# Gathering the experts' tokens for several turns at once, in split products

## The chip, the cores and the metric

The kernel runs on one core of a Trainium2 chip. The metric is the device time of one execution in microseconds (us), and smaller is better. The engines of the core are named as the profile names them: PE (TensorE, its matrix products), PEld (its loads of the stationary operand), DVE (VectorE), ACT (ScalarE), POOL (GpSimd), SP (SyncE, which here only issues the transfers of the weights, in order, on one queue).

## The reference, cut to what matters

Two layers of a small transformer work on 256 tokens of width 1024. The second layer ends with a mixture of eight experts, of which each token uses two:

```python
def moe_swiglu(h, router_w, w1, w3, w2):
    t = h.reshape(B * L, D)                       # 256 x 1024
    logits = (t @ router_w).astype(jnp.float32)
    top_v, top_i = lax.top_k(logits, TOP_K)       # 2 of 8
    gates = jax.nn.softmax(top_v, axis=-1)
    combine = jnp.einsum('tk,tke->te', gates, jax.nn.one_hot(top_i, N_EXPERTS, dtype=jnp.float32))
    out = jnp.zeros_like(t)
    for e in range(N_EXPERTS):
        out = out + combine[:, e:e + 1] * swiglu(t, w1[e], w3[e], w2[e])
    return out.reshape(B, L, D)
...
        hx = modulate(rmsnorm(x, norm_ffn_w[l]), sh2x, sc2x)
        x = x + g2x * channel_mixer(hx, l, ...)
```

An expert's `w1` and `w3` are 1024 x 3584 and its `w2` is 3584 x 1024, all in float32: 42 MiB (44 MB) an expert, 352 MB for the eight. Everything that comes ahead of the experts (modulation, mixers, the dense layer) is left as it is.

## The kernel before

The last half of the execution is `expert_pass`: eight **turns**, one for each expert, in an order that the kernel works out itself (`plan`). A turn holds the tokens of one expert in 128 slots (turns 0, 2, 4 and 6, **long**) or in 64 (turns 1, 3, 5 and 7, **short**); `TURNS` and `short(e)` say which. The busiest experts get the long turns. In the text behind this, a turn is named by its number e.

The weights of a turn come in 42 **units** of 1 MiB (`load_unit`, line 128): four chunks of the hidden width, of each first the units of `w1` and `w3` (`up`), and then, one chunk later, those of `w2` (`down`). A unit lands in one of the 8 KiB-a-partition buffers of the list `places["raw"]`. They are taken in turn: two of `hbq`, the four `rr` of the ring, `raw6` to `raw{NRM - 1}` of the pool `wm`, and for a while the places of tiles that are not needed yet (`macc` three times, `hg1` once). With NRM = 12 that is twelve buffers in the steady state. SP issues the transfer of a unit as soon as its buffer is free, so the number of buffers is how far the transfers can run ahead of the products.

In a long turn the products are float32 by splitting: ACT writes the rounded high part `hi` of a unit (line 1691), DVE the rest `lo` = raw - hi (line 1702), and PE multiplies high by high, high by low and low by high with operands of the type float32r (lines 1599, 1600 and 1603; `mm3`, lines 156 to 158, for the downs). The buffer of the unit is free when `lo` is written. In a short turn PE takes the unit as it is, in float32 (lines 1591 and 1623), in pairs of half arrays, and the buffer is free when PE has done with it; ACT and DVE have little to do then.

`fill()` and the loop behind it set the order of the instructions. For each unit: its products; then the high part of a unit two ahead (AHI = 2) and the low part of the next one (ALO = 1); then one step (`pull(behind_work[0], 1)`) of the work that waits in the list `behind_work`, first in, first out; then a step of each chunk in work (`chunk`: silu times the other branch, and the transposes of the result for the downs). All operations of `dv` and `av` keep the order in which they are written (class `InOrder`), so DVE and ACT run in the order of the program; almost all their rows in the expert part have line 177.

Ahead of its products a turn needs its tokens in its slots, transposed: `HG[e]`. `gather(e)` makes them. DVE writes a matrix `oh` (256 tokens by slots) that holds, at a token's slot, the reciprocal of its norm, and zero elsewhere; PE multiplies the residual `resid[2 + t]` by it in float32 (line 1392 for a short turn, 1405 for a long one, 16 products in each), and ACT applies scale and bias of the modulation from PSUM (and makes the high part, DVE the low one, for a long turn). `gather(e + 1)` is put into `behind_work` in the third chunk of turn e (line 1547), so the tokens of the short turns 1, 3, 5 and 7 are gathered in a long turn, and those of the long turns 2, 4 and 6 in a short one. The first turn's are gathered ahead of the pass. `finish(e, y)` brings the result back to the tokens: it transposes `oh` on PE (line 1436), takes where it is positive, and multiplies; it runs in the turn after e. In a short turn the 64 slots stand twice in `oh`, since the two halves of the result lie on partitions 0 to 63 and 64 to 127.

## Time and profile before

| what | value |
|---|---|
| median of 3 runs | 1666.03 us (1665.50 to 1667.06) |
| the profiled execution | 1667.27 us, span of its instructions 1665.5 us |
| busy share of the span: PE, DVE, ACT | 96 %, 63 %, 44 % |
| time of the chain that ended last: PE, DMA, DVE, ACT | 83 %, 6 %, 6 %, 3 % |
| moved by DMA | 479.06 MB, 288 GB/s over the span |
| DMA from about the 22nd of 40 slices on | tenths 9, 384 to 415 GB/s |

The page gives shares of the whole span, but the kernel has two parts: to about 786 us PE is busy and the DMA engines are half used (163 GB/s or so in many slices), and in the pass of the experts both are near their limits. So the stretches have to be read one by one. Times are counted from the start of the span. "Granted clock" is that of TensorE as a share of its full 2.4 GHz; 0.5 is 1.2 GHz. A busy PE is not a PE at its peak: the ends of matrix products are modelled and overlap, so the spacing of their starts is what counts.

### The profile page before, as it was taken

The numbers are of one execution on the slowest core, as the hardware profiler recorded it, in microseconds if no ns is written. First come the engines' busy times: TensorE is split into PE (matmuls) and PEld (weight loads), VectorE is DVE, ScalarE is ACT, GpSimd is POOL, SyncE is SP. The second block draws the span as 40 slices with busy tenths as digits, with TensorE's granted clock in tenths as the row PEclk, the third lists the DMA queues.
The fourth block names the chain that finished last, engine by engine and source line by source line (L and its number), as shares of the span: only waits on it lengthen the run. The fifth ranks groups of instructions, "written<-read, shape, count | busy, mean of one in ns | idle before, by whom it ended". The sixth has DMA issues, their size and how long they took to land.

```text
span 1665.5 us, 21562 instructions
## 1 busy us (share of the span) xinstructions
PE 1606.3 (96%) x8150; PEld 1159.5 (70%) x8150; DVE 1046.6 (63%) x1314; ACT 726.1 (44%) x892; POOL 27.5 (2%) x54
## 2 busy tenths in 40 slices
PE   7989999999999999999999999999999999999995
PEld 3868888788888888877786357874478844578532
DVE  3798897888567656866995127862178820588322
ACT  4733455322321347554775036741267611567201
POOL 1000000000000000000000000000000000000000
PEclk9999999999999999999999999999999999999997
DMA  9534385565666544546999999999999999999995
GB/s 372 160 102 136 96 267 163 163 189 171 189 190 201 156 128 140 174 154 240 332 357 318 415 406 413 407 406 407 409 412 409 410 390 408 410 414 406 384 405 201
DMA packets 186586, 479.06 MB, mean 288 GB/s; under 512 B 11585, under 2 KB 64961, under 8 KB 171873
## 3 DMA queue, kind: packets, MB, share of 16 engines
q1 hardware_dynamic: 185040, 473.80, 77.1%
q10 hardware_dynamic: 1074, 2.72, 0.5%
q8 instruction: 68, 1.11, 0.3%
q0 software_dynamic: 352, 1.00, 0.2%
q14 instruction: 52, 0.43, 0.1%
HBM read 476.43 MB, written 1.05 MB: 287 GB/s over the span
## 4 chain that ended last, share of the span: by engine, by line
PE 83%; DMA 6%; DVE 6%; ACT 3%; issue 1%; SPq 1%; DVEq 0%; ACTq 0%
PE h L1591 11%; PE mm L156 8%; PE mm L157 8%; PE mm L158 8%; PE h L1600 6%; PE h L1603 6%; PE h L1599 6%; PE y L156 5%; PE y L157 5%; PE y L158 5%; PE y L1623 4%; DMA rr<-moe_w 3%; PE sc L598 1%; PE sc L1570 1%; DVE lo L149 1%
## 5 line engine op out<-in xcount | busy, mean ns | idle before, releaser
L145 ACT ACTIVATE hi<-raw 128x1024 fp32r<-128x1024 f32 x127 | 134.6, 1059 | 303.2 <-PE mm L157 100.3
L177 DVE TENSOR_TENSOR rb<-raw,rb 128x2048 fp32r<-128x2048 f32 x73 | 167.1, 2290 | 80.2 <-ACT rb L177 60.5
L149 DVE TENSOR_TENSOR lo<-raw,hi 128x1024 fp32r<-128x1024 f32 x127 | 155.2, 1223 | 80.3 <-ACT hi L145 78.9
L419 DVE SCALAR_TENSOR_TENSOR rr<-rr,cs,rr 128x512 f32<-128x512 f32 x256 | 181.9, 747 | 9.6 <-DMA rr<-b_mod 4.6
L1600 PE MATMUL h<-rb,hg 128*128 128x512 f32 x448 | 177.2, 396 | 4.5 <-DVE rb L177 4.4
L156 PE MATMUL mm<-hbk,hi 128*128 128x512 f32 (+1 forms) x456 | 166.5, 366 | 1.1 <-DVE tm L837 1.0
L157 PE MATMUL mm<-hbk,hi 128*128 128x512 f32 (+1 forms) x456 | 163.6, 359 | 0.5 <-DVE hbk L310 0.5
L158 PE MATMUL mm<-hbk,lo 128*128 128x512 f32 (+1 forms) x456 | 163.8, 359 | 0.0
L177 ACT ACTIVATE rb<-raw 128x2048 fp32r<-128x2048 f32 x73 | 139.9, 1917 | 51.0 <-PE h L1603 31.8
L1591 PE MATMUL h<-raw,hgs 128*64 128x512 f32 (+1 forms) x720 | 143.4, 528 | 0.0
L177 DVE TENSOR_TENSOR sil<-sil,h 128x512 f32<-128x512 f32 (+1 forms) x44 | 29.1, 662 | 165.7 <-PE h L1591 148.5
L1599 PE MATMUL h<-rb,hg 128*128 128x512 f32 x288 | 109.1, 399 | 1.4 <-ACT rb L177 1.4
L1591 PEld LDWEIGHTS h<-raw,hgs 128*64 128x64 f32 x720 | 51.6, 137 | 77.5 <-issue 69.3
L1600 PEld LDWEIGHTS h<-rb,hg 128*128 128x128 f32 x448 | 85.1, 190 | 26.7 <-DVE rb L177 6.9
L177 DVE TENSOR_TENSOR rb<-raw,part 128x2048 fp32r<-128x2048 f32 x42 | 96.1, 2288 | 10.1 <-PE h L1600 4.6
L156 PEld LDWEIGHTS mm<-hbk,hi 128*128 128x128 f32 x456 | 85.9, 189 | 16.6 <-issue 2.7
L177 DVE TENSOR_TENSOR rb<-rr,rb 128x2048 fp32r<-128x2048 f32 x35 | 80.0, 2288 | 27.7 <-ACT rb L177 24.1
L177 ACT ACTIVATE part<-raw 128x2048 fp32r<-128x2048 f32 x42 | 80.4, 1914 | 36.2 <-DMA raw<-moe_w 16.8
L157 PEld LDWEIGHTS mm<-hbk,hi 128*128 128x128 f32 x456 | 86.0, 189 | 14.1 <-issue 1.0
L158 PEld LDWEIGHTS mm<-hbk,lo 128*128 128x128 f32 x456 | 86.0, 189 | 13.0
L1603 PE MATMUL h<-rb,hg 128*128 128x512 f32 x288 | 88.6, 393 | 2.5 <-DVE hg L177 2.5
L157 PE MATMUL y<-rb,ht 128*128 128x512 f32 x224 | 87.6, 391 | 0.0
(381 smaller groups left out, 2967.9 us busy)
## 6 DMA issues: line engine op xcount, KB each, us to landing
raw<-moe_w SPq DMA_DIRECT2D x212, 1024.0 KB
rr<-moe_w SPq DMA_DIRECT2D x110, 1024.0 KB
rr<-w_mod SPq DMA_DIRECT2D x80, 512.0 KB
raw<-ffn_w SPq DMA_DIRECT2D x72, 512.0 KB
raw<-w_in SPq DMA_DIRECT2D x32, 512.0 KB
raw<-w_out SPq DMA_DIRECT2D x23, 512.0 KB
raw<-moe_w SPq DMA_DIRECT2D x12, 512.0 KB
rb<-w_mod SPq DMA_DIRECT2D x5, 1024.0 KB
```

Source lines behind the costliest of these rows:

```text
L145: ins = nc.scalar.activation(hi, raw, AF.Copy).ins
L149: nc.vector.tensor_tensor(lo, raw, hi.bitcast(F32), op=OP.subtract)
L156: nc.tensor.matmul(ps, lh, rh, start=start, stop=False)
L157: nc.tensor.matmul(ps, lh, rl, start=False, stop=False)
L158: nc.tensor.matmul(ps, ll, rh, start=False, stop=stop)
L177: r = getattr(self.engine, name)(*args, **kw)
L419: nc.vector.scalar_tensor_tensor(accs[x], rv[:, k, :], cs[:, x * 8 + kb:x * 8 + kb + 1], accs[x], op0=OP.mult, op1=OP.add)
L1591: nc.tensor.matmul(H[i][0][x * 64:x * 64 + 64, :n], HG[e][:, k0 + j, :], hi[:, j, x * n:(x + 1) * n], start=(k0 + j == 0), stop=(k0 + j == 7))
L1599: nc.tensor.matmul(H[i][b], hgh[:, kb, :], hi[:, j, bc], start=(kb == 0), stop=False)
L1600: nc.tensor.matmul(H[i][b], hgh[:, kb, :], lo[:, j, bc], start=False, stop=False)
L1603: nc.tensor.matmul(H[i][b], hgl[:, kb, :], hi[:, j, bc], start=False, stop=(kb == 7))
L1623: nc.tensor.matmul(Y[e][0][hh * 64:hh * 64 + 64], ht[:, j0 + j, half], hi[:, j, xc], start=on, stop=off)
```

## The change

`gather` stays for the passes that run only if an expert has more tokens than slots (they are not run on these inputs), and without its branch for short turns. In the main pass `gather_group(es)` takes its place, twice: for the turns 1 to 3, put into `behind_work` in the second chunk of turn 0, and for the turns 4 to 7, in the second chunk of turn 3. It writes one matrix of zeros and ones for all their slots (64 + 64 + 128 = 256 columns, and 64 + 64 + 128 + 128 = 384), and multiplies the residual by the reciprocal norm first, split in a high part `xh` (ACT) and a low part `xl` (DVE), 256 of its columns at a time; each of the 8 blocks of 128 features then needs four products in float32r, high and low for two halves of the tokens (line 1440 of the changed kernel). ACT writes the short turns' tokens of a block in one instruction, and the high part of each long turn's; DVE writes each long turn's float32 value and its low part. The tokens of all turns of a group stay until they are used, so there are new tiles `hgs0`, `hgs1` (4 KiB a partition each) and wider `ohg0`, `ohg1`; NRM falls from 12 to 11. In `finish` the matrix of a short turn has its 64 columns once, and two products with the unit matrix for each half of the tokens (four in all) take the place of two transposes. A short turn's chunk waits one unit longer before its transposes (`yield`).

```diff
-NRM, NHM, NLM, AHI, ALO = 12, 3, 2, 2, 1
+NRM, NHM, NLM, AHI, ALO = 11, 3, 2, 2, 1
...
-            if short(e):
-                HG[e] = hg = mb.tile([128, KB, 64], F32, name="hgs", tag=f"hg{e % 2}")
-                ps = scps()
-                for k4 in range(2):
-                    for kb in range(4 * k4, 4 * k4 + 4):
-                        for t in range(2):
-                            nc.tensor.matmul(ps[:, kb * 64:(kb + 1) * 64], resid[2 + t][:, kb * 128:(kb + 1) * 128],
-                                             oh[:, t, 0:64], start=(t == 0), stop=(t == 1))
-                    yield
-                for kb in range(KB):
-                    av.activation(hg[:, kb, :], ps[:, kb * 64:(kb + 1) * 64], AF.Identity,
-                                  scale=AXM[0][:, kb:kb + 1], bias=AXM[1][:, kb:kb + 1])
-                return
...
+        def gather_group(es):
+            es = sorted(es, key=lambda e: rooms_of[e])
...
+            i = es[0] // 4
+            oh = (rxp, mo)[i].tile([128, 2, n], F32R, name="ohg", tag=f"ohg{i}")
+            for e in es:
+                cols_ = slice(starts[e], starts[e] + rooms_of[e])
+                OH[e] = oh[:, :, cols_].bitcast(F32)
+                for t in range(2):
+                    dv.tensor_scalar(oh[:, t, cols_], iota[:, 0:rooms_of[e]], PM(t, e), None, op0=OP.is_equal)
+            yield
+            ns = sum(short(e) for e in es)
+            hs = mb.tile([128, KB, ns, 64], F32, name="hgs", tag=f"hgs{i}")
...
+                hg = mb.tile([128, 2, KB, 128], F32R, name="hg", tag=f"hg{e // 2 % 2}")
+                HG[e] = hg[:, 0], hg[:, 1]
+            for k2 in range(4):
+                fc = slice(k2 * 256, (k2 + 1) * 256)
+                xh, xl = (mb.tile([128, 2, 256], F32R, name=x, tag="ys", bufs=2) for x in ("xh", "xl"))
+                for t in range(2):
+                    av.activation(xh[:, t], resid[2 + t][:, fc], AF.Copy, scale=nM.ys[2 + t])
+                    dv.scalar_tensor_tensor(xl[:, t], resid[2 + t][:, fc], nM.ys[2 + t], xh[:, t].bitcast(F32),
+                                            op0=OP.mult, op1=OP.subtract)
+                yield
+                for j in range(2):
...
+                    for x in (xh, xl):
+                        for t in range(2):
+                            nc.tensor.matmul(ps[:, :n], x[:, t, jc], oh[:, t, :], start=(x is xh and t == 0),
+                                             stop=(x is xl and t == 1))
+                    yield
+                    ak, bk = AXM[0][:, kb:kb + 1], AXM[1][:, kb:kb + 1]
+                    av.activation(hs[:, kb].rearrange("p a b -> p (a b)"), ps[:, :ns * 64], AF.Identity, scale=ak, bias=bk)
+                    h32 = mo.tile([128, 2, 128], F32, name="h32", tag="oht")
+                    for k, e in enumerate(longs):
+                        pe_ = ps[:, starts[e]:starts[e] + 128]
+                        av.activation(HG[e][0][:, kb, :], pe_, AF.Identity, scale=ak, bias=bk)
+                        dv.tensor_scalar(h32[:, k], pe_, ak, bk, op0=OP.mult, op1=OP.add)
+                        dv.tensor_tensor(HG[e][1][:, kb, :], h32[:, k], HG[e][0][:, kb, :].bitcast(F32), op=OP.subtract)
...
             for t in range(2):
-                nc.tensor.transpose(ps[:, t * 128:(t + 1) * 128], oh[:, t, :], ident)
+                tc_ = slice(t * 128, (t + 1) * 128)
+                if short(e):
+                    for o in (0, 64):
+                        nc.tensor.matmul(ps[o:o + 64, tc_], oh[:, t, :], ident, start=True, stop=True)
+                else:
+                    nc.tensor.transpose(ps[:, tc_], oh[:, t, :], ident)
...
+            if PM is by_turn and (e, c) in ((0, 1), (3, 1)):
+                behind_work.append(gather_group(range(1, 4) if e == 0 else range(4, 8)))
             yield
             flat = sil.rearrange("p b c -> p (b c)")
             if short(e):
+                yield
                 ps = scps()
```

Two places show how the instructions move. The first is DVE in turn 0, in the units after its second chunk. In the names, `rb1` and `rb3` are the two buffers of low parts, each of these rows splits one unit; `ht` is the transposed result for the downs. Before:

```order
L177 TENSOR_TENSOR rb3_7043<-raw_7014,rb2_7016 128x2048
L177 TENSOR_TENSOR ht_6996<-sc_7022,ht_6996 128x512
L177 TENSOR_TENSOR rb1_7063<-rr0_7039,part_7041 128x2048
L177 TENSOR_TENSOR rb3_7083<-rr1_7059,rb0_7061 128x2048
L177 TENSOR_TENSOR rb1_7101<-raw_7079,rb2_7081 128x2048
L177 TENSOR_TENSOR rb3_7119<-raw_7097,part_7099 128x2048
```

The same units in the changed kernel:

```order
L177 TENSOR_TENSOR rb3_7058<-rr0_7021,rb2_7023 128x2048
L177 TENSOR_TENSOR ht_7003<-sc_7037,ht_7003 128x512
L177 TENSOR_TENSOR rb1_7083<-rr1_7054,part_7056 128x2048
L177 TENSOR_SCALAR h32_7086<-sc_7060,ac110_4860,modc_3844 128x128
L177 TENSOR_TENSOR hg_7028<-h32_7086,hg_7028 128x128
L177 TENSOR_TENSOR rb3_7113<-raw_7079,rb0_7081 128x2048
L177 TENSOR_SCALAR h32_7116<-sc_7090,ac110_4860,modc_3844 128x128
L177 TENSOR_TENSOR hg_7028<-h32_7116,hg_7028 128x128
L177 SCALAR_TENSOR_TENSOR xl_7121<-resid2_1867,rsy_6458,xh_7120 128x256
L177 SCALAR_TENSOR_TENSOR xl_7121<-resid3_1869,rsy_6507,xh_7120 128x256
L177 TENSOR_TENSOR rb1_7142<-raw_7109,rb2_7111 128x2048
```

Between two splits there are now two small operations of the long turn 2's tokens, and in every third unit two more that make `xl`; this goes on over 15 splits.

The second place is SP's queue of weight transfers in turn 0, from one use of the buffer `rr3` to the next use of `rr2` (`raw` are the buffers of `hbq` and `wm`, `head` is the place of `macc`). Before:

```order
L128 DMA raw_6990<-moe_w2 128x2048
L128 DMA raw_7014<-moe_w2 128x2048
L128 DMA rr0_7039<-moe_w1 128x2x1024
L128 DMA rr1_7059<-moe_w1 128x2x1024
L128 DMA raw_7079<-moe_w1 128x2x1024
L128 DMA raw_7097<-moe_w1 128x2x1024
L128 DMA raw_7115<-moe_w3 128x2x1024
L128 DMA raw_7133<-moe_w3 128x2x1024
L128 DMA raw_7156<-moe_w3 128x2x1024
L128 DMA raw_7174<-moe_w3 128x2x1024
L128 DMA head_7192<-moe_w2 128x2048
L128 DMA rr2_7210<-moe_w2 128x2048
```

In the changed kernel:

```order
L128 DMA raw_6968<-moe_w2 128x2048
L128 DMA raw_6990<-moe_w2 128x2048
L128 DMA rr0_7021<-moe_w2 128x2048
L128 DMA rr1_7054<-moe_w1 128x2x1024
L128 DMA raw_7079<-moe_w1 128x2x1024
L128 DMA raw_7109<-moe_w1 128x2x1024
L128 DMA raw_7138<-moe_w1 128x2x1024
L128 DMA raw_7161<-moe_w3 128x2x1024
L128 DMA raw_7189<-moe_w3 128x2x1024
L128 DMA head_7223<-moe_w3 128x2x1024
L128 DMA rr2_7246<-moe_w3 128x2x1024
```

One `raw` is gone from the cycle, and each buffer comes round one unit earlier.

## Rows read from the trace of the kernel before

**Rows 1.** Stretches: us, busy us (count) by engine, granted clock, DMA share, GB/s.

```profile
786.00:903.00 117.00, 115.96 (x537) 96.15 (x538) 100.60 (x87) 81.62 (x60) 0.00 (x0) 1.00 0.92 333
...
992.00:1112.00 120.00, 119.61 (x546) 94.80 (x546) 100.30 (x63) 83.34 (x62) 0.00 (x0) 1.00 1.02 410
1112.00:1204.00 92.00, 89.62 (x447) 39.23 (x447) 14.64 (x18) 13.42 (x22) 0.00 (x0) 1.00 1.02 406
...
1548.00:1642.00 94.00, 91.57 (x437) 37.09 (x435) 19.40 (x31) 10.35 (x14) 0.00 (x0) 1.00 1.00 392
```

**Rows 2.** Stretches of 5 us, at the ends of long turns.

```profile
880.00:885.00 5.00, 5.00 (x24) 4.13 (x23) 3.94 (x2) 3.88 (x6) 0.00 (x0) 1.00 0.71 224
...
1120.00:1125.00 5.00, 5.00 (x26) 1.73 (x24) 0.00 (x0) 0.06 (x1) 0.00 (x0) 1.00 1.00 335
...
1335.00:1340.00 5.00, 5.00 (x25) 1.99 (x25) 0.00 (x0) 0.00 (x0) 0.00 (x0) 1.00 0.81 283
1340.00:1345.00 5.00, 5.00 (x26) 1.63 (x24) 0.33 (x1) 2.76 (x3) 0.00 (x0) 1.00 0.99 346
...
1550.00:1555.00 5.00, 5.00 (x20) 2.42 (x18) 0.00 (x0) 0.00 (x0) 0.00 (x0) 1.00 0.94 373
1555.00:1560.00 5.00, 5.00 (x26) 1.73 (x24) 0.00 (x0) 0.00 (x0) 0.00 (x0) 1.00 0.86 247
1560.00:1565.00 5.00, 5.00 (x26) 1.64 (x24) 2.15 (x1) 4.19 (x3) 0.00 (x0) 1.00 0.94 365
```

**Rows 3.** Waits of SP's queue, 780 to 1665 us: total, times, longest.

```profile
SPq L128 <- DVE rb L177: 275.4, 115, 12.2
```

**Rows 4.** The chain that ended last: start, us, what.

```profile
1084.77 1.73 PE sc L1392 x16
...
1632.61 9.49 DMA raw<-moe_w
```

**Rows 5.** PE in order of time around 701 us: products of 256 columns.

```profile
700.87 0.28 PE L156 MATMUL mm<-hbk,hi 128*128 128x256 f32 x1
700.99 0.28 PE L157 MATMUL mm<-hbk,hi 128*128 128x256 f32 x1
```

**Rows 6.** DVE in order of time in turn 0; in brackets idle before.

```profile
849.00 2.29 DVE L177 TENSOR_TENSOR rb<-raw,part 128x2048 fp32r<-128x2048 f32 x1 [0.43 <-PE h L1600]
851.72 2.29 DVE L177 TENSOR_TENSOR rb<-raw,rb 128x2048 fp32r<-128x2048 f32 x1 [0.43 <-PE h L1600]
...
868.52 0.98 DVE L177 TENSOR_SCALAR oh<-rt,turns,rsy 128x64 f32<-128x64 f32 x4
```

**Rows 7.** DVE groups by form: count, busy us, mean ns, idle before.

```profile
L310 DVE TENSOR_TENSOR hbk<-h,hbk 128x256 fp32r<-128x256 f32 x32 | 12.2, 419 | 2.7 <-ACT hbk L309 2.6
...
L177 DVE SCALAR_TENSOR_TENSOR macc<-sc,turns,macc 128x512 f32<-128x512 f32 x28 | 20.1, 745 | 1.5 <-PE sc L1462 0.8 <-PE sc L1493 0.7
...
L177 DVE TENSOR_SCALAR h<-g,ac,modc 128x128 f32<-128x128 f32 x8 | 2.6, 404 | 2.1 <-PE g L1188 2.1
...
L177 DVE TENSOR_TENSOR c<-lg 128x64 f32<-128x64 f32 x4 | 0.7, 220 | 0.0
```

**Rows 8.** PE in order of time: a finish's transposes, and first products of long turns.

```profile
1023.10 0.38 PE L1436 MATMUL sc<-sqc,oh 128*128 128x128 f32 x2
...
992.60 0.50 PE L1600 MATMUL h<-rb,hg 128*128 128x512 f32 x1 [0.39 <-DVE rb L177]
...
1426.48 0.65 PE L1600 MATMUL h<-rb,hg 128*128 128x512 f32 x1 [1.60 <-DVE rb L177]
```

**Rows 9.** Stretches of 5 us at the starts of turns 2, 4 and 6.

```profile
990.00:995.00 5.00, 4.61 (x21) 2.58 (x18) 4.47 (x2) 3.71 (x3) 0.00 (x0) 1.00 1.02 406
...
1205.00:1210.00 5.00, 3.15 (x10) 1.68 (x7) 3.76 (x2) 3.70 (x3) 0.00 (x0) 0.82 1.03 410
1210.00:1215.00 5.00, 5.00 (x19) 3.99 (x19) 3.31 (x3) 2.99 (x2) 0.00 (x0) 0.84 1.03 409
...
1425.00:1430.00 5.00, 3.52 (x9) 2.74 (x10) 3.72 (x2) 3.57 (x2) 0.00 (x0) 0.67 1.02 409
```

26 lines of the change are left out of this document (18 added, 8 removed).

## Prediction

> **What bounds the kernel now.** I read the span by stretches first, since the page's shares mix two parts. Only the pass of the experts is touched, from about 786 us on. In it PE looks full everywhere, so I looked at what the DMA engines do beside it. In the long turn 2 they run at a share of 1.02 and 410 GB/s: the transfers never stop. In the short turns they sink to 406 GB/s (turn 3) and 392 (turn 7, to its end), and in turn 0 to 333 [rows 1]. So from turn 2 on the pass is a stream of transfers at 410 GB/s with a few dips, and turn 0 is slower because PE is.
>
> Stretches of 5 us show where the dips lie: right after each long turn [rows 2]. Against 410 GB/s they cost (410 - 335) x 5 / 410 = 0.9 us after turn 2, (127 + 64) x 5 / 410 = 2.3 us after turn 4, and (37 + 163 + 45) x 5 / 410 = 3.0 us after turn 6: 6.2 us together. The reason is in SP's waits: SP stands 275.4 us, 115 times, until DVE has written the low part of a unit and so freed its buffer [rows 3]. In a long turn PE is slower than the transfers, which run ahead until every buffer is full. Then a transfer starts only when a buffer comes free. In the short turn behind it PE is faster, empties the buffers and waits for a transfer at the turn's end; the last 9.49 us of weights at the end of the pass are such a wait [rows 4].
>
> From this follows how costs count. Where the buffers are full, the stream has got as far as PE plus the buffers; a us that PE or DVE loses in a long turn then is a us lost at the end, and so is a MiB of lookahead (1.049 MB / 410 GB/s = 2.6 us). Where PE waits for transfers, at the ends of short turns, PE's work is free.
>
> **The change part by part**, in us at the end.
>
> *One buffer less.* The cycle of buffers is one shorter in the rows of SP's queue. At the end of turn 0 the buffers are full (224 GB/s at 880 us [rows 2]), so the stream leaves turn 0 a MiB further behind: **+2.6**. It takes the same from the lookahead at the ends of turns 2, 4 and 6, counted below.
>
> *Turn 0, PE.* It loses the gather of turn 1, two pieces of 1.73 us, 3.5 us [rows 4]. It gains 8 blocks of 4 products over 256 columns, whose starts in float32r lie 0.12 us apart [rows 5]: 32 x 0.12 = 3.8 us. Net **+0.4**, including some reordering.
>
> *Turn 0, DVE.* DVE is nearly full there. In a unit PE takes 2.72 us (the starts of two splits, 849.00 and 851.72 us) and DVE idles 0.43 [rows 6]. New on DVE: 8 operations of 256 columns for xl, 8 of 128 columns from PSUM for h32, 8 of 128 columns for the low part, 6 for the matrix. No row has these forms exactly. For xl the nearest are 419 ns (two tensors, 256 columns) and 745 ns (the same operation on 512): I take 0.45 us, near the first. For h32 the row is 404 ns, and eight of them are 2.6 us busy: 0.33 each. For the low part the bounds are 220 ns (64 columns) and 419 (256): 0.30 [rows 7]. With 1.6 us for the matrix that is 3.6 + 2.6 + 2.4 + 1.6 = 10.2 us, less the 0.98 us of the old matrix, which came later in turn 0 [rows 6]. They are spread over 15 units, in which DVE has 15 x 0.43 = 6.5 us of idle time and the 3.8 us that PE now takes longer: 10.3. The two are level. The low part of the next unit is asked for one unit ahead, and most of an overrun in one unit is made up in the next. The stall of PE is between 0 (the small operations all fit) and 4 us (the xl at the upper end, 8 x 0.3 = 2.4, and an order that never fits): I take **+1**. ACT's new work, 24 small instructions, has more room (82 us busy of 117 [rows 1]) and runs two units ahead: 0.
>
> *Turns 2, 4 and 6.* Each loses the gather of a short turn, 3.5 us of PE on the path that fills the buffers. In `finish` four products with the unit matrix replace two transposes of 0.38 us together [rows 8]; by the spacing of the gather's products (1.73 / 16 = 0.11 us a record, two records a product) they take at most 0.9 us: between 0 and +0.6, I take +0.3. One MiB less of lookahead is +2.6. Net 0.6 earlier in each, and all three dips are deeper than that: **-1.8**.
>
> On the transposes a rule of the Trainium skill speaks against the change: Perfetto Trace Analysis, section Transposes, wants transposes done as such and not as ordinary products. No run here shows a product in this place; the rule gives no price, and the bound above from rows stands.
>
> *Turns 1, 3, 5 and 7.* PE loses the gather of a long turn in three of them and some waits for silu; turn 3 gains 32 products of 384 columns (between 0.12 and 0.23 us each, some 5.5 us). DVE and ACT are almost idle (14.64 and 13.42 us of 92 [rows 1]). PE waits for transfers at the end of these turns, so all this is worth nothing; turn 3's addition is hidden by the same wait, and if that cover were gone it would cost its excess over the gather that leaves, about 1.5 us.
>
> *The clock after the wait.* PE reaches turn 2 with a wait of only 0.39 us, turn 6 with 1.60 [rows 8]. At turn 2 the granted clock stays 1.00 (2.4 GHz); at turns 4 and 6 it falls toward 1.2 GHz, with a mean of 0.82 and 0.84 over 10 us and of 0.67 over 5 us [rows 9]: 0.18 x 5 + 0.16 x 5 = 1.7 us of PE, and 0.33 x 5 = 1.7 us. With less work in turn 1 and a stream that is 4 us later, PE will wait longer ahead of turn 2 and the fall should come there too: **+1.7**, bounds 0 (it doesn't come) and +5 (it comes and lasts longer at all three). The dips of the three turns then come out level, as those after 4 and 6 are now.
>
> The Trainium skill says on this (TensorE: Matmul & The Clock Gate, HAM oscillation) that waits for DMA between groups of products bring the clock back to half rate. The rows at turns 4 and 6 agree, and by that rule the upper bound would be the likelier one.
>
> *The tail* from the last unit on (1642 us) is the same work; the products of the last `finish` lie in the wait for the last transfers: 0.
>
> Sum: 2.6 + 0.4 + 1.0 - 1.8 + 1.7 = +3.9. Against the profiled execution (1667.27 us, its span 1665.5 and 1.8 around it) that is 1671.2. The median of the runs is 1.2 us below that execution, so I forecast 1666.0 + 3.9 = **1669.9 us**.
>
> **The rivals.**
>
> *Slower by DVE.* In turn 0 the small operations don't fit between the splits; the price is the 4 us above instead of 1, and with the longer wait behind it the upper end of the clock's cost. 1666.0 + 2.6 + 0.4 + 4 - 1.8 + 4 = 1675. For it: DVE is at 100.60 of 117 us already [rows 1]. Against it: the gather also gives DVE time, as PE is busy with it. It decides from the point at which a unit's new DVE work is above 0.43 us plus PE's new work in that unit, in most units.
>
> *No fall of the clock, no stall.* 1666.0 + 2.6 + 0.4 - 1.8 = 1667.2, no change that can be told. For it: at the start of turn 2 the granted clock stayed at 1.00 [rows 9], and the small operations fit by their sum.
>
> *Faster: the lookahead isn't what I think.* If eleven buffers carry the stream as well as twelve (the transfers being held by something else than full buffers in turn 0), the 3.2 us that each of the turns 2, 4 and 6 saves go against the dips: 0.9 + 2.3 + 3.0 = 6.2 us less, with 0.4 and 1 more in turn 0: 1661. For it: in turn 0 there are stretches with a DMA share near 1 and under 400 GB/s, which full buffers alone don't explain. Against it: SP's waits for freed buffers, and the dips right at the ends of long turns.
>
> **How the numbers follow.** A measurement of this kernel can tell about 0.2 %, 3.3 us: faster is below 1662.7, slower above 1669.4. The forecast case, 1668 to 1672, has 0.48, two thirds of it above 1669.4; slower by DVE 0.15; no fall and no stall 0.25; faster 0.12. So faster 0.12, the same 0.16 + 0.25 = 0.41, slower 0.32 + 0.15 = 0.47. The range must leave out no more than 2 in 10: from 1664 (all of the faster case below it, with what little of the others) to 1676 (the far half of the DVE case above it, and longer falls of the clock).
>
> **What the profile after would show.** One buffer less: the transfers of turn 0 reach any given unit with the same distance in PE's time, but the dips right after turns 2, 4 and 6 are no shallower than now by more than a us. DVE in turn 0: idle time before the splits gone in about 15 units, and PE waits of its products (L1600 of before) for the low part of under 2 us in all. Turns 2, 4 and 6: shorter by about 3 us from first to last product where the clock is equal. Clock: a granted clock under 1 at the start of turn 2. The prediction is wrong if turn 0 grows by more than 5 us, if turn 2 starts no later than now, or if the stream has gaps at the ends of short turns, where I count on none.

## The result and the profile after

The changed kernel takes **1675.65 us** (median of 6 executions, 1672.04 to 1677.73) against 1665.97 us for the kernel before (6 executions, 1665.38 to 1667.06): a ratio of 1.0056, with a 95 % interval of 1.0043 to 1.0069. So it is slower, as forecast, but by 9.7 us and not by 3.9. The time lies inside the range (1664 to 1676), at its upper edge. Run once more beside the experiments, it took 1674.1 us against 1667.09 us, 1.0050 (1.0036 to 1.0064).

The profiled execution of the changed kernel is the fastest of its six: 1672.04 us, span 1670.3 us. These are four of its stretches, one long turn at the start, the short turn behind it, and the long turns 2 and 6; the columns are those of [rows 1].

```profile
786.00:903.00 117.00, 114.09 (x525) 93.93 (x526) 109.76 (x117) 89.19 (x80) 0.00 (x0) 1.00 0.89 322
903.00:988.00 85.00, 80.61 (x396) 33.67 (x397) 11.42 (x13) 8.76 (x11) 0.00 (x0) 1.00 0.99 387
992.00:1112.00 120.00, 115.84 (x507) 89.29 (x508) 96.85 (x56) 81.88 (x54) 0.00 (x0) 0.99 1.02 410
1426.00:1548.00 122.00, 118.34 (x517) 92.21 (x516) 99.92 (x58) 84.27 (x56) 0.00 (x0) 0.97 1.02 410
```

Against [rows 1], turn 0 moves 322 GB/s instead of 333, and DVE is busy for 109.76 of 117 us there instead of 100.60. From turn 2 on the stream runs at 410 GB/s as before. In both of these turns PE is now busy for some 4 us less than the stretch is long: it waits. The chain of waits shows for what, at the start of turn 2. Its columns are the start, the duration and what it was:

```profile
975.99 18.43 DMA raw<-moe_w
994.42 0.02 issue
994.44 1.92 ACT rb L177
996.36 0.02 issue
996.38 2.31 DVE rb L177
998.69 0.04 issue
998.73 0.79 PE h L1644
```

Turn 2 begins when its first unit has landed, at 994.42 us, and been split: its first low part is multiplied at 998.73 us, 1.59 us after PE was ready for it. Before, that was at 992.60 us with a wait of 0.39 us [rows 8]. The stretches of 5 us around the starts of turns 2, 4 and 6 show the clock (last column but two):

```profile
995.00:1000.00 5.00, 2.00 (x5) 1.37 (x6) 3.35 (x2) 3.97 (x4) 0.00 (x0) 0.84 1.03 412
1000.00:1005.00 5.00, 5.00 (x19) 4.00 (x19) 3.53 (x2) 3.39 (x2) 0.00 (x0) 0.82 1.03 410
...
1210.00:1215.00 5.00, 5.00 (x25) 1.49 (x21) 2.00 (x1) 3.56 (x3) 0.00 (x0) 1.00 1.02 408
...
1425.00:1430.00 5.00, 2.37 (x8) 0.64 (x4) 1.31 (x1) 2.89 (x3) 0.00 (x0) 0.85 1.03 409
1430.00:1435.00 5.00, 3.97 (x9) 3.14 (x10) 3.36 (x3) 3.11 (x2) 0.00 (x0) 0.50 1.03 410
```

It falls at turn 2, where it did not before, stays at 1.00 at turn 4, where it fell before, and falls further at turn 6 [rows 9]. These are the dips behind the long turns 2, 4 and 6, to be read against [rows 2]:

```profile
1125.00:1130.00 5.00, 5.00 (x26) 1.73 (x24) 0.00 (x0) 0.52 (x2) 0.00 (x0) 1.00 0.97 344
...
1340.00:1345.00 5.00, 5.00 (x26) 1.62 (x24) 0.00 (x0) 0.26 (x1) 0.00 (x0) 1.00 1.00 384
...
1555.00:1560.00 5.00, 5.00 (x25) 1.95 (x26) 0.00 (x0) 0.00 (x0) 0.00 (x0) 1.00 0.79 273
```

The dip behind turn 4 has all but gone, the other two are nearly as deep as before. So of what the stream has lost when turn 0 ends it gets back no more than 2.4 us (dips of 5.6 us together before, of 3.2 now, by the table below). Against a second profile of the kernel before, whose dips are 2.6 us (e9), it gets back nothing. The end of turn 0 is where the larger part of the time went.

### The profile page after: what moved, and what is told of

It reads as the page before. It is cut to its first block, busy times and chain, and to the rows that moved or that the text cites. A ratio compares the mean times of both kernels' runs of the same rounds, so it can differ in the third digit from the quotient of the medians.

```text
span 1670.3 us, 21359 instructions
## 1 busy us (share of the span) xinstructions
PE 1598.7 (96%) x8014; PEld 1143.3 (68%) x8014; DVE 1061.9 (64%) x1364; ACT 723.5 (43%) x886; POOL 27.5 (2%) x54
## 3 DMA queue, kind: packets, MB, share of 16 engines
HBM read 476.43 MB, written 1.05 MB: 286 GB/s over the span
## 4 chain that ended last, share of the span: by engine, by line
PE 83%; DMA 6%; DVE 6%; ACT 3%; issue 1%; SPq 1%; POOL 0%; DVEq 0%; ACTq 0%; POOLq 0%
PE h L1635 10%; PE mm L156 8%; PE mm L157 8%; PE mm L158 8%; PE h L1644 6%; PE h L1647 6%; PE h L1643 6%; PE y L156 5%; PE y L157 5%; PE y L158 5%; PE y L1667 4%; DMA raw<-moe_w 3%; DMA rr<-moe_w 1%; PE sc L598 1%; DVE lo L149 1%
## 5 line engine op out<-in xcount | busy, mean ns | idle before, releaser
L177 DVE TENSOR_TENSOR rb<-raw,rb 128x2048 fp32r<-128x2048 f32 x71 | 162.3, 2289 | 71.6 <-ACT rb L177 59.8
L177 ACT ACTIVATE rb<-raw 128x2048 fp32r<-128x2048 f32 x71 | 136.2, 1918 | 89.3 <-DMA raw<-moe_w 41.5
L1635 PE MATMUL h<-raw,hgs 128*64 128x512 f32 (+1 forms) x632 | 130.2, 541 | 3.5 <-DMA raw<-moe_w 3.5
L177 DVE TENSOR_TENSOR rb<-rr,rb 128x2048 fp32r<-128x2048 f32 x38 | 86.9, 2289 | 36.1 <-ACT rb L177 31.6
L1635 PEld LDWEIGHTS h<-raw,hgs 128*64 128x64 f32 x632 | 45.4, 137 | 76.4 <-issue 65.8
L157 PEld LDWEIGHTS mm<-hbk,hi 128*128 128x128 f32 x456 | 86.1, 189 | 14.1 <-issue 1.0
L158 PEld LDWEIGHTS mm<-hbk,lo 128*128 128x128 f32 x456 | 86.1, 189 | 13.1
L177 ACT ACTIVATE sil<-h 128x512 f32<-128x512 f32 (+1 forms) x44 | 24.9, 574 | 154.4 <-PE h L1635 145.9
L1635 PE MATMUL h<-rr,hgs 128*64 128x512 f32 (+1 forms) x392 | 84.7, 543 | 1.8 <-DMA rr<-moe_w 1.8
```

What stands on the lines that cost most here:

```text
L157: nc.tensor.matmul(ps, lh, rl, start=False, stop=False)
L158: nc.tensor.matmul(ps, ll, rh, start=False, stop=stop)
L177: r = getattr(self.engine, name)(*args, **kw)
L1635: nc.tensor.matmul(H[i][0][x * 64:x * 64 + 64, :n], HG[e][:, k0 + j, :], hi[:, j, x * n:(x + 1) * n], start=(k0 + j == 0), stop=(k0 + j == 7))
```

## One table for all profiles

Fourteen profiles were taken in the end (the experiments are told in the next section). For each kernel the table says when PE was done with the up-products (those with `w1` and `w3`) of turn 0, when 290 MB of the 479 MB were still to be moved (which is in turn 1 or just behind, where the stream runs freely again), and the difference of the two. The first is the end of the last such product in the timeline of PE, the second is added up from the GB/s of the stretches of 5 us. The dips are the sums of (411 - GB/s) x 5 / 411, with their signs, around the ends of turns 2, 4 and 6, in us; which stretch is the first and the last moves a value by 0.3 us or so (in e2, whose dips begin ahead of the turns' ends, by more). The durations are those from the first to the last up-product of the turns 0, 2, 4 and 6.

| kernel | buffers, last use of `macc` | ups of turn 0 end | 290 MB left | difference | dips | ups of turns 0, 2, 4, 6 |
|---|---|---|---|---|---|---|
| before | 12, 42nd unit | 892.1 | 930.5 | 38.4 | 0.9, 2.0, 2.7 | 109.6, 113.8, 116.5, 116.6 |
| e9, before again | 12, 42nd | 894.2 | 932.6 | 38.5 | 0.2, 2.2, 0.2 | 109.6, 113.2, 116.6, 115.0 |
| e4 | 12, 42nd | 892.4 | 930.9 | 38.4 | 2.5, 0.4, 2.0 | 109.6, 109.5, 109.5, 109.5 |
| e5 | 12, 42nd | 894.6 | 933.0 | 38.5 | 0, 1.4, 0 | 110.0, 111.4, 114.7, 111.9 |
| e8 | 12, 42nd | 897.2 | 935.4 | 38.2 | 0, 0, 1.1 | 111.6, 110.1, 110.9, 114.8 |
| e11 | 12, 29th | 897.0 | 937.3 | 40.3 | 1.2, 0.3, 2.0 | 111.2, 115.0, 115.0, 116.6 |
| e6 | 11, 51st | 896.9 | 937.2 | 40.3 | 2.5, 1.0, 1.6 | 112.0, 114.1, 111.1, 114.3 |
| e10 | 11, 51st | 894.7 | 935.0 | 40.3 | 2.0, 0.1, 2.4 | 110.5, 114.6, 110.1, 114.9 |
| **after** | 11, 39th | 894.8 | 937.5 | 42.7 | 1.0, 0.2, 2.0 | 110.5, 113.4, 110.1, 113.9 |
| e1, after again | 11, 39th | 897.3 | 939.8 | 42.5 | 1.0, 0.2, 2.1 | 112.1, 113.4, 110.1, 114.0 |
| e7 | 11, 39th | 896.6 | 939.3 | 42.8 | 2.7, 0.7, 2.4 | 112.0, 114.7, 110.1, 114.5 |
| e3 | 11, 39th | 898.2 | 941.1 | 42.8 | 1.3, 0.4, 2.3 | 112.1, 110.1, 110.6, 110.1 |
| e12 | 11, 39th | 894.8 | 937.3 | 42.6 | 1.3, 2.5, 1.2 | 110.1, 113.5, 114.6, 113.4 |
| e2 | 11, 39th | 894.1 | 936.9 | 42.8 | 4.8, 6.1, 6.2 | 109.6, 117.0, 117.4, 117.8 |

The column of differences takes three values, whatever the gather is: 38.2 to 38.5 with the buffers of before, 40.3 with one unit less of lookahead at the end of turn 0, 42.5 to 42.8 with two. That is the main finding, and the experiments stand behind it one by one.

## The experiments

**e1, the changed kernel again, and e2, one buffer less alone.** e2 is the kernel before with one line of the change:

```
-NRM, NHM, NLM, AHI, ALO = 12, 3, 2, 2, 1
+NRM, NHM, NLM, AHI, ALO = 11, 3, 2, 2, 1
```

> The changed kernel once more, to see an execution nearer to its median of 1675.7 us; its profiled execution took 1672.0. Its runs list granted clocks of 0.986 to 0.990, the longer the time the lower the clock, while before has 0.992. Theory (the clock): the extra time of the longer executions lies where PE waits for transfers in short turns, with a granted clock well under 1 there, and the starts of the turns behind come late; time 1672 to 1678. Rival (turn 0: the order of the small operations on DVE and ACT): the extra time lies between 786 and 906 us, turn 0 is more than 2 us longer than the 118 us of the first profile. Rival (the part ahead of the experts): the first products of turn 0 come later than at 788 us.

> The kernel before with NRM = 11 and nothing else: one buffer less. Theory (full buffers at the end of every long turn): the stream loses one MiB of lookahead, 2.6 us, at the ends of turns 0, 2, 4 and 6, since all four are followed by a dip already: 4 x 2.6 = 10.4 us, 1674 to 1678, with deeper dips after each long turn. With the clock falling more at the longer waits, up to 1680. Rival (the transfers are held by something else than full buffers): no more than 2.6 us, under 1669.

Measured: e1 1674.1 us, e2 **1684.74 us** (1.0104, interval 1.0082 to 1.0127) against 1667.09 us. In the profile of e1 the pass starts at 785.2 us (after: 784.3), and turn 0's up-products last 112.1 us instead of 110.5, with a granted clock of 0.89 and 0.77 at their start; turns 2, 4 and 6 are as long as in the first profile. So its extra microseconds lie at the start of the pass and in a fall of the clock at turn 0, and not in the waits of the short turns, where the theory had put them. The buffer alone, in e2, costs 17.6 us, far more than the 10.4 that four units of 2.6 us would make. With eleven buffers each, the change's gather is then 10.6 us faster than the old one (1684.74 - 1674.1). So the change is the sum of a gather that wins and a buffer that loses more. (The whole gather of the change with twelve buffers was not run; a part of it was, in e5.)

Where e2 loses it stands in the table: 4.3 us at the end of turn 0 (42.8 - 38.5), and 4.6, 3.9 and 6.0 us more dip than e9, in all 18.8 us. Its turns 2, 4 and 6 last 117.0 us or more, about the length of a turn of before in which the clock fell, and it falls at the start of each (0.55, 0.58 and 0.50 in the lowest stretches of 5 us; in e9 at turn 4 alone, 0.66). How these 14.5 us divide between the missing unit and the clock was not followed up. The 4.3 us are worth a look, since turn 0 of e2 has exactly PE's work of before. Here are the 150 us from the end of attention to the start of turn 1, e9 first, then e2 (last column: GB/s):

```profile
780.00:930.00 150.00, 145.97 (x689) 111.58 (x690) 112.01 (x111) 91.86 (x75) 0.00 (x0) 1.00 0.93 341
```

```profile
780.00:930.00 150.00, 145.89 (x691) 111.60 (x691) 111.92 (x110) 91.84 (x75) 0.00 (x0) 1.00 0.90 329
```

The order of the buffers explains the 4.3 us. Beside the steady buffers, the place of `macc` takes a unit three times. With twelve buffers the third of these is the 42nd unit of the pass, with eleven the 39th. PE is done with all but the last two long units of turn 0 at the 40th. So with twelve buffers the stream may then be 13 units ahead, with eleven only 11: the edit of one buffer takes two units of lookahead there.

**e6, one of the two units given back.** The changed kernel with the place of `macc` used once more:

```
-MA = 2
+MA = 3
```

> The changed kernel with MA = 3: the place of macc takes a unit's weights four times instead of three, the last time in turn 1. In the kernel before, the third of these units is the 42nd, and it is still ahead of PE when turn 0 ends; with eleven buffers it is the 39th, so at the end of turn 0 the stream is two units behind, not one. Theory (the two units of 2.6 us are the larger part of what turn 0 loses): one of them comes back, the stream behind turn 0 is about 2.6 us earlier, and the time 1671 to 1672, against 1674.1 for the change. Rival (turn 0 is held by DVE, or finish of turn 0, which now has to wait for the place, gives it back): 1674 to 1676.

Measured: **1672.18 us** (1.0031, interval 1.0020 to 1.0041, against 1666.27), and in the table 40.3 instead of 42.5 to 42.8. The row over the same 150 us shows it too. First the changed kernel, then e10, which has this edit too and whose turn 0 runs with the same clock (last column: GB/s):

```profile
780.00:930.00 150.00, 145.88 (x686) 111.26 (x686) 119.04 (x135) 97.63 (x91) 0.00 (x0) 1.00 0.90 327
```

```profile
780.00:930.00 150.00, 145.94 (x685) 111.17 (x685) 118.99 (x134) 97.65 (x91) 0.00 (x0) 1.00 0.92 333
```

6 GB/s over 150 us are 0.9 MB, one unit within the rounding of the row. The ratio is 0.0019 below e1's, some 3 us, in line with it; the two intervals overlap.

**e11, one unit taken from the kernel before.** The kernel before, twelve buffers, with `MA = 1`: only the lookahead at the end of turn 0 changes, by one unit.

> The kernel before, twelve buffers, with MA = 1: the place of macc takes a unit's weights twice instead of three times. So at the end of turn 0 the stream is one unit shorter of lookahead (the 51st unit is the last that may start when PE is done with the 39th, instead of the 52nd), and from turn 1 on nothing differs. Theory (two such units cost 4.2 to 4.3 us of stream in the profiles with eleven buffers, and one cost 1.9 in e6): the stream behind turn 0 is 2.1 us later, and 1.5 to 2.5 us of it reach the end: 1668 to 1669.5, against 1666.3 to 1667.4 for the kernel before. Rival (what is lost in turn 0 is made up by shallower dips behind the long turns, as the late start in the second profile of before was): 1666 to 1667.5.

(The units in this expectation are counted from zero.)

Measured: 1669.41 us against 1668.05 us, 1.0004 (0.9994 to 1.0013). The trace shows the unit (40.3 instead of 38.5), so its price in the stream holds: **1.9 us**. What of it reaches the end can't be told from these runs; the interval allows 2.2 us and allows nothing.

So by the table the first unit of lookahead at the end of turn 0 costs 1.8 to 2.1 us and the second 2.2 to 2.5, together less than the 5.1 us that the transfers of two units take at 410 GB/s. The packets of the transfers show why. 14 us behind the last up-product of turn 0 the kernel before has 299.2 MB left to move, e6 and e11 300.2, the changed kernel and e2 301.2: that is one unit and two (1.05 MB each) almost in full, 2.5 and 4.9 us. Right behind it the kernel before loses time of its own. These are the 16 us from that moment on, before first, then after:

```profile
906.10:922.10 16.00, 16.00 (x77) 7.59 (x74) 5.18 (x3) 4.79 (x4) 0.00 (x0) 1.00 0.98 353
```

```profile
908.80:924.80 16.00, 16.00 (x75) 7.53 (x72) 5.18 (x3) 4.20 (x3) 0.00 (x0) 1.00 0.98 365
```

12 GB/s over 16 us are 0.2 MB, 0.5 us. SP's issues at that moment, before first, then after (start, duration; x2 is two issues), fit it:

```profile
905.37 0.37 SPq L128 DMA_DIRECT2D raw<-moe_w  x1
908.80 2.09 SPq L128 DMA_DIRECT2D rr<-moe_w  x2
```

```profile
908.07 0.39 SPq L128 DMA_DIRECT2D rr<-moe_w  x1
909.78 2.09 SPq L128 DMA_DIRECT2D raw<-moe_w  x2
```

Before, the 54th unit is issued at 905.37 us and the 55th 3.4 us later, since the place of `macc`, which held the 42nd, has just dropped out and SP waits for the next buffer of the list; after, the 52nd and the 53rd are 1.7 us apart. So a unit of lookahead is worth the time of its transfer here, less what the stream of the kernel before loses anyway.

**e5, the gather without its price.** To see what the gather is worth at twelve buffers, only the short turns are gathered together, all four at once in turn 0, and their tokens (8 KiB a partition) lie where the second long turn's were; the long turns' gather stays where it was in the kernel before.

```diff
-NRM, NHM, NLM, AHI, ALO = 11, 3, 2, 2, 1
+NRM, NHM, NLM, AHI, ALO = 12, 3, 2, 2, 1
...
-            hs = mb.tile([128, KB, ns, 64], F32, name="hgs", tag=f"hgs{i}")
+            hs = mb.tile([128, KB, ns, 64], F32, name="hgs", tag="hg1")
...
-            if c == 2 and e + 1 < NE and PM is not by_turn:
+            if c == 2 and e + 1 < NE and (PM is not by_turn or not short(e + 1)):
                 behind_work.append(gather(e + 1))
...
-            if PM is by_turn and (e, c) in ((0, 1), (3, 1)):
-                behind_work.append(gather_group(range(1, 4) if e == 0 else range(4, 8)))
+            if PM is by_turn and (e, c) == (0, 1):
+                behind_work.append(gather_group((1, 3, 5, 7)))
```

> The gather of the change without its price in buffers: only the four short turns are gathered together (256 columns, split products, one matrix of zeros and ones), in turn 0, and their tokens lie where the second long turn's lay (hg1, 8 KiB); the long turns 2, 4 and 6 are gathered one by one in the short turn ahead, as before; twelve buffers, no extra unit of waiting ahead of a short turn's transposes. Theory (what the change lost is the buffer, what it won is the 3.5 us of PE that each of the turns 2, 4 and 6 no longer spends on a gather): turn 0's up-products last 109.6 + 0.3 to 1 us, those of turns 2, 4 and 6 about 110.3 us where the clock stays full (before 113.8) and about 113.5 where it falls; the dips of 0.9, 2.3 and 3.0 us after them go; 1660 to 1663 us, against 1667 for the kernel before. Rival (it is the split gather itself, its DVE work in turn 0 and the four products of finish that cost): 1667 to 1672. On the later start of the pass (784.3 to 786.1 us in the four profiles with eleven buffers, 782.5 and 782.8 in the two with twelve): if the number of buffers sets it, here 782.5 to 783; if it is chance, it may be either.

Measured: **1666.57 us** against 1666.27 us, 0.9999 (0.9989 to 1.0009). No loss, and no gain either: the theory was nearly right on the turns and wrong on the total. Turns 2 and 6 last 111.4 and 111.9 us, turn 4 114.7 with a fall of the clock; the dips are 0, 1.4 and 0. But that is little to win. The kernel before has dips of 5.6 us in the profile that I had read, and of 2.6 us in its second profile (e9). Of e5's smaller dips, 0.4 us go to a longer turn 0, and PE now comes too early at turn 4, waits for the first unit and loses its clock:

```profile
1208.92 0.73 PE L1641 MATMUL h<-rb,hg 128*128 128x512 f32 x2 [2.57 <-ACT rb L177]
1211.24 0.80 PE L1642 MATMUL h<-rb,hg 128*128 128x512 f32 x1 [1.59 <-DVE rb L177]
```

(Timeline of PE in e5; in brackets what it waited for, and how long.) With 5 MB left the stream is 1.2 us ahead of e9's (1630.0 and 1631.2 us), and the last product of turn 7 ends level with e9's (1642.4 and 1642.5 us); where that last microsecond goes was not followed up.

**e12, the same with eleven buffers.**

> The kernel of e5 (short turns gathered at once) with eleven buffers. Theory (a buffer costs two units at the end of turn 0, 4.3 us, and behind each long turn only what the 3.5 us of the lost gather don't cover): 4.3 + 3 x (2.6 - 3.5, no less than 0 where there is no dip left) and some falls of the clock, 1670 to 1674, so nearly the changed kernel's 1674 to 1675.6 though the long turns are gathered as before. Rival (a buffer costs the 17.6 us that it cost the kernel before, whatever the gather): 1683 to 1685.

Measured: **1674.88 us** against 1668.05 us, 1.0049 (1.0033 to 1.0064), just above the theory's 1670 to 1674. That is the changed kernel's loss, though the long turns are gathered as before. Against e5 the ratio is 0.50 % or 8.3 us higher; the table has 4.1 us of it at the end of turn 0 and 3.6 us in the dips (5.0 us together against 1.4). So a buffer costs this gather half of what it costs the old one. That part of the missing lookahead isn't needed where PE needs 3.5 us less in a long turn is my reading of it, not shown by itself. The row over the same 150 us, e5 first, then e12:

```profile
780.00:930.00 150.00, 145.93 (x689) 111.64 (x689) 115.13 (x122) 95.88 (x83) 0.00 (x0) 1.00 0.93 340
```

```profile
780.00:930.00 150.00, 145.93 (x687) 111.69 (x688) 115.21 (x123) 95.91 (x83) 0.00 (x0) 1.00 0.89 328
```

PE, DVE and ACT do the same in both; the stream moves 1.8 MB less.

**e4, the old gather moved into short turns.** The kernel before, twelve buffers, with the short turns 3, 5 and 7 gathered by its own `gather` in the short turn ahead, and the change's extra unit of waiting ahead of a short turn's transposes.

```diff
-            if c == 2:
-                behind_work.append(gather(e + 1) if e + 1 < NE else residual() if base == 0 else iter(()))
+            if c == 2 and PM is not by_turn:
+                behind_work.append(gather(e + 1) if e + 1 < NE else residual() if base == 0 else iter(()))
+            elif c == 2 and e == NE - 1:
+                behind_work.append(residual())
+            elif c == 2 and e == 0:
+                behind_work.append(gather(1))
+            elif c == 1 and short(e) and e + 1 < NE:
+                behind_work.append(gather(e + 1))
+                behind_work.append(gather(e + 2))
```

> The kernel before with twelve buffers and its own gather, but the tokens of the short turns 3, 5 and 7 gathered in the short turn ahead (two halves of one tile), and the wait of one unit ahead of a short turn's transposes as in the change. Nothing of the split products. Theory (full buffers at the ends of long turns are what a PE microsecond is worth there): 3.5 us less of PE in turns 2, 4 and 6 against dips of 0.9, 2.3 and 3.0 us: 4 to 6 us faster, 1660 to 1662. Rival (the pair of a long and a short turn is as long as PE's work in it, wherever that stands): the same as before, 1665 to 1667.

Measured: **1670.34 us** against 1667.09 us, 1.0019 (1.0007 to 1.0030), slightly slower, which neither theory nor rival had. This shows that a step of my reading was too coarse: PE's time in a short turn is not free. The long turns got shorter as expected, 109.5 us all three, with no fall of the clock. But the up-products of the short turns 1, 3 and 5 now take 86.1, 89.4 and 91.1 us instead of 80.1, 83.4 and 83.3, and PE reaches turn 2 at 997.9 us, 17.6 us after the moment when 270 MB are left; in e9 it is 12.0 us (993.6 and 981.6 us). So it is 5.6 us later against the stream. In a short turn PE catches up with the transfers only at its very end (the waits of 0.39 and 1.60 us in [rows 8]), so all beyond that wait delays the long turn.

**e3, PE kept busy ahead of the long turns.** The changed kernel with float32 products that nobody reads, one of 256 columns in each unit of parts of turns 1, 5 and 7, and four of 512 columns ahead of turns 2 and 6:

```diff
+        def keep_busy(n, cols_):
+            ps = scps()
+            for _ in range(n):
+                nc.tensor.matmul(ps[:, :cols_], ident, resid[2][:, :cols_], start=True, stop=True)
```

> The changed kernel with products that nobody reads, float32, in the waits of PE: one of 256 columns behind each unit in the second half of turns 1, 5 and 7, four of 512 columns ahead of the first unit of turns 2 and 6. They add work and take nothing away. Theory (the clock): the granted clock stays at 1 through the ends of turns 1, 5 and 7 and the starts of turns 2 and 6, the long executions go, and the time falls to 1667 to 1671 in all runs, by 4 to 7 us against the changed kernel. Rival (the clock is only a sign of the waits, and something else makes the executions long): 1675 or more, since the products only add work.

Measured: **1682.6 us** (1.0088, interval 1.0064 to 1.0111). The clock did stay at 1.00, and the long turns last 110.1, 110.6 and 110.1 us instead of 113.4, 110.1 and 113.9. But the products cost more than that. Timeline of PE, ahead of turn 2:

```profile
992.96 1.88 PE L1625 MATMUL sc<-resid,sqc 128*128 128x256 f32 x4
996.64 1.98 PE L1625 MATMUL sc<-resid,sqc 128*128 128x512 f32 x4
1000.42 1.12 PE L1625 MATMUL sc<-resid,sqc 128*128 128x512 f32 x2
1003.34 0.73 PE L1652 MATMUL h<-rb,hg 128*128 128x512 f32 x2
```

They put off the first product of turn 2 to 1003.34 us. In the changed kernel it came 9.9 us after the moment with 270 MB left (996.4 and 986.5 us); here that moment is 990.0 us, so it could have come at 999.9. The 3.4 us of delay are what the kept clock gives back. In turn 7 they lengthen the up-products from 80.8 to 88.9 us, which the end pays. So this run says what a kept clock is worth in a turn, and nothing on the total.

**e8 and e10, a smaller dose.** Two float32 products of 512 columns ahead of the first product of the turns 2, 4 and 6 of e5 (e8), and of the turns 2 and 6 of e6 (e10).

```diff
+                if PM is by_turn and e in (2, 4, 6) and c == 0 and i == 0 and k0 == 0:
+                    ps = scps()
+                    for _ in range(2):
+                        nc.tensor.matmul(ps, ident, resid[2][:, :512], start=True, stop=True)
```

> The kernel of e5 (short turns gathered at once, twelve buffers) with two float32 products of 512 columns, about 1.9 us whose result nobody reads, ahead of the first product of each of the turns 2, 4 and 6, where PE waits for the first weights of the turn. In e5 PE waited there 1.0, 2.57 + 1.59 and 0.72 + 1.59 us, and the clock fell in turn 4: its up-products lasted 114.7 us, against 111.4 and 111.9 in the turns 2 and 6. Theory (the gather's gain in e5 is given back by a clock that falls more often; its mean in e5 is 0.990, in the kernel before 0.993): all three turns at a granted clock of 1.00 and 110 to 112 us, at most 1 us lost where PE waited less than the products take, 1663.5 to 1665.5 against 1666.6. Rival (the stream has no dips left to give, so neither the gather nor the clock is worth anything any more): 1666 to 1668.

> The kernel of e6 (the change, with the place of macc taken once more) with the same two products ahead of the turns 2 and 6, where PE waits 2.56 + 1.59 us for the first weights. In e6 the up-products of these turns last 114.1 and 114.3 us with a clock that falls, and 110.1 in the changed kernel's turn 4, where it doesn't. Theory (a fall costs 3 to 4 us of PE, and of that the depth of the dip behind the turn at the end, 2.5 and 1.5 us in e6): both turns at 110 to 111 us, the dips behind them gone, 1668.5 to 1670.5 against 1672.2. Rival (the dips behind the long turns are not made by the clock): 1671.5 to 1673.

Measured: e8 1666.68 us against 1667.43 us, 0.9997 (0.9987 to 1.0007); e10 1673.49 us, 1.0036 (1.0024 to 1.0049), no better than e6 and outside both of its ranges. The expectation that the clock would stay failed: PE runs the two products at once and then waits as before. Timeline and stretches of e10 at turn 2:

```profile
993.80 0.73 PE L1647 MATMUL h<-rb,hg 128*128 128x512 f32 x2 [2.38 <-ACT rb L177]
996.13 0.79 PE L1648 MATMUL h<-rb,hg 128*128 128x512 f32 x1 [1.60 <-DVE rb L177]
```

```profile
995.00:1000.00 5.00, 3.87 (x9) 3.10 (x10) 3.37 (x2) 3.22 (x2) 0.00 (x0) 0.50 1.03 410
1000.00:1005.00 5.00, 5.00 (x19) 3.99 (x19) 3.62 (x2) 2.84 (x2) 0.00 (x0) 0.82 1.02 406
```

In e8 it stayed at turns 2 and 4 and fell at turn 6 (0.75 and 0.57). e8's time is that of its rival: it has dips of 1.1 us in all, and is still no faster than the kernel before. (In this profile the smaller dips make up for most of a pass that starts 0.9 us later than e9's and a turn 0 that is 2.0 us longer.) Behind turn 0 the stream has no more than these 1.1 us left to give.

**e7, the transposes at once.** The changed kernel without the extra unit of waiting (`yield`) in the chunks of a short turn.

> The changed kernel without the extra unit of waiting ahead of a short turn's transposes. Theory (in the changed kernel PE waits for transfers at the ends of turns 1 and 5 anyway, so the waits for silu that come back are hidden there, and only turns 3 and 7 can lose them): 1674 to 1677, against 1674.1. Rival (all PE time of a short turn counts, since PE only just catches up with the transfers): 4 turns with 3 waits of about 0.8 us, 1680 to 1684.

Measured: 1675.08 us, 1.0047 (1.0033 to 1.0060), not to be told from the change. This part of the change does nothing that can be measured.

**e9, the kernel before again.**

> The kernel before, unchanged, for a second profile of it. In eight of the ten profiles so far the pass of the experts starts 1.8 to 3.6 us later than in the profile of before, with the same instructions ahead of it; the later start goes with a granted clock under 1 near 125 us. If it is chance, the start here is 782.5 or 784.2 to 786; if it hangs on the kernel, 782.5.

Measured: 1666.09 us, span 1664.3 us, and a start of the pass (first up-product) at 784.64 us. The code ahead of the pass is the same in all these kernels, and still the pass started at 782.45 us in the profile that I had read, and between 784.2 and 786.1 us in twelve of the thirteen others. The difference arises here, before first, then before again (last column but two: the clock):

```profile
120.00:130.00 10.00, 6.57 (x26) 4.43 (x25) 9.93 (x18) 2.56 (x5) 1.05 (x2) 1.00 0.50 159
```

```profile
120.00:130.00 10.00, 6.58 (x24) 3.64 (x22) 9.37 (x16) 2.79 (x5) 1.05 (x2) 0.83 0.49 158
```

PE stands still for 3.4 us near 121 us, and in all profiles it is busy for 6.57 or 6.58 of these ten microseconds; in two (before and e4) the clock stayed, in the other twelve it fell. So it is chance, and e9 is the fairer mate for the profile after: 784.64 and 784.26 us at the start.

The Trainium skill (TensorE: Matmul & The Clock Gate, Part 1, the HAM clock gate) calls the number of slow products at a kernel's start variable from run to run. That is said of the start; these two profiles of one kernel show the like for a wait further in: 1.00 and 0.83 in the same ten microseconds.

## Why the prediction was right in sign and too small

Point by point, the profile after against e9, in us of the stream (the times at which 290, 200, 110 and 5 MB were left: after 937.5, 1157.9, 1377.7 and 1636.4; e9 932.6, 1152.4, 1374.2 and 1631.2).

*One buffer less, at the end of turn 0: forecast +2.6, measured +4.2 (42.7 - 38.5).* This is the step that failed: the mechanism, full buffers, was right, the number of units was not. I wrote that the stream leaves turn 0 "a MiB further behind". It leaves it two units behind, because the place of `macc` goes out three units earlier when the cycle is shorter. Both things could be read from the code: the list of places and the count of its uses. Two units are 5.1 us by their transfers; 0.9 of that did not count, most of it because the stream of the kernel before loses time of its own right behind (e11).

*Turn 0, PE +0.4 and DVE +1: measured +0.9 together.* From the first to the last up-product turn 0 lasts 110.5 us instead of 109.6. In e5 and e12, whose group has the same 32 products but less than half of the added DVE work (115.1 us busy in the row of 150 us, against 119.0 after and 112.0 in e9), it lasts 110.0 and 110.1: 0.4 or 0.5 for PE (its 32 products take 3.8 us from start to start, the old gather 3.4), and 0.4 or 0.5 that come with the tokens of the long turn. The durations that I had bounded for DVE stand in the groups of turn 0 (count, busy us, mean ns, idle time before):

```profile
L177 DVE SCALAR_TENSOR_TENSOR xl<-resid,rsy,xh 128x256 fp32r<-128x256 f32 x8 | 3.5, 477 | 0.0
L177 DVE TENSOR_SCALAR h<-sc,ac,modc 128x128 f32<-128x128 f32 x8 | 3.3, 408 | 0.8 <-ACT hg L177 0.5
L177 DVE TENSOR_TENSOR hg<-h,hg 128x128 fp32r<-128x128 f32 x8 | 2.3, 292 | 0.3
L1644 PE MATMUL h<-rb,hg 128*128 128x512 f32 x110 | 43.5, 395 | 0.9 <-DVE rb L177 0.8
```

0.45, 0.33 and 0.30 us were taken; 0.48, 0.41 and 0.29 came. The last row says that PE waited 0.8 us for a low part in all of turn 0. The kernel before has this wait too, 0.81 us at 823.6 us, so the +1 that I put down to a stall of PE behind DVE did not come as such a stall; how the tokens of the long turn cost 0.4 or 0.5 us is not shown. The rival of a turn 0 held by DVE did not come.

*Turns 2, 4 and 6: forecast -1.8, together with the clock's +1.7 about 0; measured +0.3.* The stream's lag behind e9 goes from 4.9 us to 5.5, 3.5 and 5.2 us behind the three turns. (Against the first profile of the kernel before, with its deeper dips, it goes from 7.0 to 4.3 us: -2.7.) That the sum came out near the forecast is in part luck, as both of its large terms were too small. In e2, with the buffer alone, the stream loses 13.7 us in these turns (1649.2 us with 5 MB left, 18.0 behind e9, less the 4.3 of turn 0), where I had taken 3 x 2.6 = 7.8; so with eleven buffers the gather gives back 13.4, where I had taken 3 x 3.2 = 9.6. The PE time of the gather was right: with no fall of the clock and no wait of over 0.4 us for the first low part a long turn lasts 113.2 or 113.8 us with a short turn's gather and 109.5 to 110.6 without it, 3.5 us or so less, as taken from the two pieces of 1.73 us. The clock fell at turn 2, as forecast: (0.16 + 0.18) x 5 = 1.7 us; with the wait of 1.59 us for the first low part, which I had not counted, that makes the 3.3 us by which turn 2 is longer than turn 4. (The waits that I had read in [rows 8] were each the last of two. At turn 6 before, PE had also waited 1.10 us for the high part; at turn 2 it had not.) That it stayed up at turn 4 was not forecast. There the second group's products, which I had called worth nothing, keep PE busy in turn 3: its up-products take 88.1 us instead of 83.4, and PE comes to turn 4 without a wait. That PE's work in a short turn is free was too coarse a rule (e4). At turn 6 it fell deeper, (0.15 + 0.50 + 0.03) x 5 = 3.4 us, a part of it while PE waited. In e12, which has no second group, turn 4 waits and lasts 114.6 us.

*Finish.* The bound of 0 to 0.6 us for the four products with the unit matrix held. The group of eight records (two for each of the four) in the profile after and the group of two transposes in that of before, from the timelines of PE:

```profile
1030.77 0.66 PE L1473 MATMUL sc<-sqc,ohg 128*64 128x128 f32 x8
```

```profile
1023.10 0.38 PE L1436 MATMUL sc<-sqc,oh 128*128 128x128 f32 x2
```

They take 0.28 us more. The rule of the Trainium skill (Perfetto Trace Analysis, Transposes), that a transpose be done as one, has the right sign and a price that doesn't count here.

*The tail: forecast 0.* From the last product of turn 7 to the end it takes 22.9 us in the profile after, 21.8 in e9, 22.3 in that of before, and 21.4 to 23.4 in the others: no difference beyond this scatter.

The sum of these is 4.2 + 0.9 + 0.3, less 0.4 for the earlier start, 5.0 in the stream, and the spans differ by 6.0 us (1670.3 and 1664.3); the rest is the tail. The sum forecast was 3.9; the mis-sized buffer is 1.6 us of what was missed and does not make 9.7 of it. The medians differ by more than the profiles, 7.0 and 9.7 us. The executions of the changed kernel have a mean clock of 0.985 to 0.991, those of the kernel before in the same runs 0.990 to 0.995. One such fall is seen at the first products of turn 0, in six of the fourteen profiles (e1: 0.89 and 0.77 in the two stretches from 785 us on), and lengthens turn 0 by some 1.6 us. It hits e8 and e11 with twelve buffers as well as e1, e3, e6 and e7. Whether the change makes it likelier can't be said from so few. The executions of which the clock is known say how far it goes with the time. At a mean clock of 0.990 the changed kernel took 1672.04 and 1674.08 us and the kernel before 1667.03 to 1670.93 (13 executions, median 1668.52): 4.5 us apart, near the sum above. At 0.986 the changed kernel took 1677.17 to 1678.15 us (three executions). So the further microseconds of the medians go with the lower clock. Whether it makes them, or the waits for a late stream make both, stays open.

What I said would show the steps right or wrong: the distance in turn 0 was to stay the same but for one unit, and that was wrong; the dips were to be no shallower by more than a us, which fails at turn 4; DVE's idle time before the splits of turn 0 is gone in ten units, not in 15; the waits for the low part, the shorter long turns and the clock at turn 2 came as said. The stream has no gaps at the ends of short turns.

None of the kernels here is faster than the kernel before by more than the interval; e5, e8 and e11 are level with it.

## What to carry to other kernels

When a change pays with a buffer, simulate the list of places unit by unit for the old and the new count, up to each point where the stream is held; places that drop out after a number of uses make one buffer count twice. Price a unit of lookahead by its transfer, and take off what the stream loses at that point anyway: here two units of 2.6 us cost 4.2. And read two profiles of the kernel before ahead of counting what dips could give: here one showed 5.6 us of them and the other 2.6, with spans of 1665.5 and 1664.3 us.
